# Float32 side matmuls of a fused decoder layer gathered into every second unit of main matmuls, and the last output tile sent in two halves

## The chip, the cores and the metric

The kernel runs on one core of a Trainium2 chip. The metric is the device time of one execution in microseconds (us). A core has TensorE (matmuls, into PSUM banks), VectorE, ScalarE, GpSimd and SyncE; here SyncE does nothing but issue DMAs.

## What is computed

One inference step of a one-layer decoder with three parallel groups of heads, for 256 prompt tokens and 64 sample tokens (8 requests of 8), all in float32:

```python
def finish(x, y_conv, y_swa, y_x, w_out, g_mlp, w_up, w_down):
    x = x + jnp.concatenate([y_conv, y_swa, y_x], axis=-1) @ w_out
    a = jnp.square(jax.nn.relu(rmsnorm(x, g_mlp) @ w_up))
    return x + a @ w_down
...
b, u, q, k, v, qx = mixer_projections(xs, g_mix[l], w_in[l], g_q_swa[l], g_k_swa[l], g_q_x[l])
u_ext = jnp.concatenate([cache_conv[l], u], axis=1)
y_conv = b * short_conv(u_ext, conv_w[l])
y_swa, k_buf, v_buf = swa_sample(q, k, v, cache_swa_k[l], cache_swa_v[l], sinks[l], rel_bias_table)
y_x = cross_attention(qx, cache_mem_k[l], cache_mem_v[l])
s_conv.append(u_ext[:, -(CONV_K - 1):])
xs = finish(xs, y_conv, y_swa, y_x, w_out[l], g_mlp[l], w_up[l], w_down[l])
```

The model width is 2048, the MLP 8192 wide; a head has 128 columns. `y_conv` is a gated convolution over three tokens, `y_swa` attention over a window of 128 tokens (8 heads on 2 key heads), `y_x` attention of 4 heads over 256 memory tokens. The prompt goes through the same layer with its own memory, and its keys and values are outputs. So are the convolution's last two inputs, and the caches of the window moved on by 8 tokens.

## The kernel before

**Main work.** All 320 tokens lie side by side as columns, the model width on partitions. A weight matrix is cut into groups of 512 output columns (four PSUM banks `mm` of 128 rows by 320 columns) and pieces of 512 KB (two blocks of 128 rows). A float32 product is made of three matmuls with shortened operands: a piece arrives in tile `raw` (4 buffers, `load_piece`, SyncE's queue), ScalarE rounds it into `wh`, VectorE makes the rest `wl` = `raw` - `wh` (4 buffers each, `split_piece`); the activations lie in the same two parts, S0h and S0l, S1h and S1l. The right to load the next piece into a `raw` buffer comes with the end of that `wl` split, and the load is issued there in program order.

A **unit** (`run_unit`) is 12 main matmuls of 320 columns (6 of 512 for the memory keys and values). A group has 16 units, or 8 for the half groups of `w_out`. The groups follow in a fixed order: memory queries (C_X), keys and values (C_K), the prompt's memory keys and values, window queries (two groups), the convolution's three parts (C_C, C_H, C_B), then `w_out` in two passes of four half groups, then `w_up` and `w_down` in four rounds of four and four groups. The first pass of `w_out` folds its PSUM banks into the residual x: `pre_out` issues, just before unit 4 of its first half group, four DMAs of 640 KB that bring x into the `lx` tiles, and `part_evac` (VectorE) adds each finished bank to them. The fifth bank, first of the next half group, can be written once the first bank is folded.

**Side work.** Attention, norms and the convolution's leftovers are "jobs": generators that a scheduler (`Side`) advances by a step after each unit (`boundary`: first the evacuations that are due, then the `wl` split, then `side.step()`). `yield n` means "come back n units later". A job waits for its tiles by a model of the engines' times (`Pace`, `after`), and takes a PSUM bank `ax` (four of them) by `bank`. So side matmuls stand in **batches** between two units: plain float32 matmuls, transposes, and those of `cross_sample`, where each head has 32 output rows and the four heads sit in four column tiles of the array. `cross_sample` runs through four requests b for the memory keys and four for the values, each with two loaded tiles of 128x512. All issues of engines are recorded through one helper, so they carry line 166 in the profile; tiles tell them apart.

**What a unit may ask for.** `side.until(needs)` runs extra scheduler steps until the jobs named are done. Unit 4 of the first `w_out` half group asks for "conv" and "convout". The job "convout" makes eight small copies on VectorE and stores them with a DMA on GpSimd. GpSimd's queue keeps program order: behind that store come the two copies of the old window caches, `out_old_k` and `out_old_v` (960 KB each, from DRAM to DRAM, issued by `pre_late`).

**The end.** `down_evac` adds the last banks to x; the tiles of the last group go out one by one on SyncE.

Of the kernel before, what the change touches and what calls it, by code (L numbers as in the profile page):

```python
# [12 lines left out]
ALU = mybir.AluOpType  # L13
AX = mybir.AxisListType

P = 128
D = 2048
KT = 16
# [4 lines left out]
T = TP + TS  # L23
# [224 lines left out]
def trunk_step(ctx: ExitStack, tc: tile.TileContext, I, O):  # L248
    nc = tc.nc
    pace = Pace()  # L250
    side = Side(NW2, pace)
    pace.dram = {a.name for a in list(I.values()) + list(O.values())}
    pe, act, dve = (Paced(pace, n, e) for n, e in (("pe", nc.tensor), ("act", nc.scalar), ("dve", nc.vector)))
    pool, sp = Paced(pace, "pool", nc.gpsimd), Paced(pace, "dma", nc.sync)
# [13 lines left out]
    ax = Slots(axp, "ax", 4, pace.idle)  # L268
# [3 lines left out]
    def after(*tiles):  # L272
        while not pace.ready(tiles):
            yield 1

    def bank():
        return ax.need([P, 512])

    def zt(cols=336):
        return zs.need([P, 336])  # L280

    def sm(n=8):
        return smp.tile([P, 8], F32, name="sm", tag="sm")
# [6 lines left out]
    def half():  # L290
        return w2.need([P, 512])
# [65 lines left out]
    def mean_over(bk, y, scale):  # L357

        hi = yield from zs.need([P, T], F32R)
        lo = yield from zs.need([P, T], F32R)  # L360
        act.activation(out=hi, in_=y, func=AF.Copy)
        dve.tensor_tensor(out=lo, in0=y, in1=hi.bitcast(F32), op=ALU.subtract)
        yield 1
        yield from after(lo)
        pe.matmul(out=bk[:, 0:T], lhsT=scale, rhs=hi, start=True, stop=False)
        pe.matmul(out=bk[:, 0:T], lhsT=scale, rhs=lo, start=False, stop=True)
        yield 1
        zs.put(hi, lo)

    def newton_terms(y, a, mean):  # L370
        act.activation(out=y, in_=mean, func=AF.Ln, bias=eps)
        act.activation(out=y, in_=y, func=AF.Exp, scale=-0.5)
        act.activation(out=a, in_=y, func=AF.Square)
        yield from after(a)
        dve.scalar_tensor_tensor(out=a, in0=mean, scalar=EPS, in1=a, op0=ALU.add, op1=ALU.mult)
# [161 lines left out]
    def mean_rsqrt(out, sq):  # L537

        yield from after(sq)
        bk = yield from bank()  # L540
        yield from mean_over(bk, sq, mean_d)
        y = yield from zt()
        yield from newton_terms(y[:, 0:T], out, bk[:, 0:T])
        ax.put(bk)
        dve.tensor_scalar(out=y[:, 0:T], in0=y[:, 0:T], scalar1=-0.5, scalar2=None, op0=ALU.mult)
        dve.scalar_tensor_tensor(out=out, in0=out, scalar=-3.0, in1=y[:, 0:T], op0=ALU.add, op1=ALU.mult)
        zs.put(y)
# [52 lines left out]
    def start_head(name, ps, gain, dest):  # L600
        early = "rb" not in side.flags
        home = w2 if early else zs
        z = home.must([P, 336])
        if early:
            side.held += 1
            act.activation(out=z[:, 0:T], in_=ps, func=AF.Copy)
        else:
            dve.tensor_tensor(out=z[:, 0:T], in0=ps, in1=rb, op=ALU.mult)

        def gen():  # L610
            if early:
                while "rb" not in side.flags:
                    yield 1
                dve.tensor_tensor(out=z[:, 0:T], in0=z[:, 0:T], in1=rb, op=ALU.mult)
            while side.now < turn[0] or turn[1] == 2:
                yield 1
            turn[0] = side.now + 2
            turn[1] += 1
            y = yield from zt()
            yield from after(z)  # L620
            act.activation(out=y[:, 0:T], in_=z[:, 0:T], func=AF.Square)
            yield 1
            yield from after(y)
            bk = yield from bank()
            yield from mean_over(bk, y[:, 0:T], mean_h)
            a = yield from zt()
            yield from newton_terms(y[:, 0:T], a[:, 0:T], bk[:, 0:T])
            ax.put(bk)
            dve.scalar_tensor_tensor(out=z[:, 0:T], in0=z[:, 0:T], scalar=gain, in1=y[:, 0:T],
                                     op0=ALU.mult, op1=ALU.mult)  # L630
            zs.put(y)
            dest(lambda out, v: dve.scalar_tensor_tensor(out=out, in0=v(a), scalar=-3.0, in1=v(z),
                                                         op0=ALU.add, op1=ALU.mult))
            zs.put(a)
            home.put(z)
            side.held -= int(early)
            turn[1] -= 1

        side.add(name, gen())

    def prompt_cols(t):
# [167 lines left out]
    def cross_sample(f):  # L809
        todo = [(n, b) for n in ("cmk", "cmv") for b in range(4)]  # L810
        queue = []

        def load():
            if todo:
                n, b = todo.pop(0)
                pair = []
                for i in range(2):
                    t = yield from half()
                    src = I[n][f * 4 + b, i]
                    sp.dma_start(out=t, in_=src.rearrange("p h k -> p (h k)") if n == "cmk" else src)  # L820
                    pair.append(t)
                queue.append(pair)

        qm = st["qxm"][f]
        for _ in range(2):
            yield from load()
        sb = yield from bank()
        for b in range(4):
            cur = queue.pop(0)
            yield from after(*cur)  # L830
            for h in range(XH):
                pe.matmul(out=sb[h * 32:(h + 1) * 32, 0:MEM], lhsT=qm[:, h * P + b * 32:h * P + b * 32 + 32],
                          rhs=cur[h // 2][:, (h % 2) * MEM:(h % 2 + 1) * MEM], start=b == 0, stop=b == 3,
                          tile_position=(0, h * 32), skip_group_check=True)
            w2.put(*cur)
            yield from load()
        yield 1
        p = yield from zt()
        den = sm()
        yield from cross_softmax([(p[:, 0:MEM], sb[:, 0:MEM])], den)  # L840
        ax.put(sb)
        yield from after(p)
        pm = []
        for kb in range(2):
            t = yield from half()
            pool.memset(t, 0.0)
            pm.append(t)
        bk = yield from bank()
        for kb in range(2):
            pe.transpose(bk[:, kb * P:(kb + 1) * P], p[:, kb * P:(kb + 1) * P], ident)  # L850
        yield 1
        for kb, t in enumerate(pm):

            dve.tensor_copy(out=bass.AP(tensor=t.tensor, offset=t.offset, ap=[t.ap[0], [P + NS, 4], [32, XH], [1, NS]]),
                            in_=bk[:, kb * P:(kb + 1) * P].rearrange("p (h b t) -> p b h t", h=XH, b=4))
        ax.put(bk)
        zs.put(p)
        yield from after(*pm)
        ob = yield from bank()
        for b in range(4):  # L860
            cur = queue.pop(0)
            yield from after(*cur)
            for kb in range(2):
                for h in range(XH):
                    c = h * 32
                    pe.matmul(out=ob[c:c + 32, 0:P], lhsT=pm[kb][:, b * P + c:b * P + c + 32],
                              rhs=cur[kb][:, h * P:(h + 1) * P], start=b == 0 and kb == 0, stop=b == 3 and kb == 1,
                              tile_position=(0, c), skip_group_check=True)
            w2.put(*cur)
            yield from load()  # L870
        yield 1
        w2.put(*pm)
        o = yield from zt()
        act.activation(out=o[:, 0:P], in_=ob[:, 0:P], func=AF.Copy)
        ax.put(ob)
        yield from after(o)
        bk = yield from bank()
        pe.transpose(bk[:, 0:P], o[:, 0:P], ident)
        yield 1
        zs.put(o)  # L880
        c = TP + f * 32
        yield from put_mix(lambda m: m[:, 12:16, c:c + 32], bk[:, 0:P].rearrange("p (h q) -> p h q", h=XH))
        ax.put(bk)
        w2.put(qm)
        side.held -= 1
# [321 lines left out]
    def down_evac(g, last):  # L1207
        def f(m, ps):
            a = acc[g][:, m, :]
            dve.tensor_tensor(out=a, in0=ps, in1=a, op=ALU.add)  # L1210
            if last and (g == 3 or m == 3):
                c = slice(m, m + 1) if g == 3 else slice(0, 4)
                sp.dma_start(out=O["yT"][:, 4 * g + c.start:4 * g + c.stop, :], in_=acc[g][:, c, :])
        return f
# [44 lines left out]
    bk = ax.must([P, 512])  # L1259
# [74 lines left out]
```

## Time and profile before

| | before |
|---|---|
| median of 3 runs | 1319.12 us (1319.0 to 1320.92) |
| the profiled execution: its time, its span | 1319.92 us, 1317.9 us |
| TensorE busy | 1311.2 us, 99%, 8938 instructions |
| VectorE busy | 669.4 us, 51% |
| ScalarE busy | 538.7 us, 41% |
| GpSimd busy | 17.4 us, 1% |
| granted TensorE clock, mean of the span | 0.999 of full speed |
| read from HBM, written | 211.53 MB, 7.65 MB |

A busy share is an average over the whole span. Side work lies in the first quarter of it, so the stretches (busy time of each engine from one time to another) say more than the table. The chain of waits is the chain of work that ended last, followed back from the end; on TensorE it runs in pieces, main (`mm`) and side (`ax`) by turns. A timeline lists instructions with their start, their duration and, in brackets, the idle time of the engine ahead of them and what ended it. Matmuls of TensorE overlap: one of 320 columns shows some 0.31 us in a timeline, though one starts every 0.147 us.

### The profile page before, as it was taken

To read this page: it belongs to the slowest core of one execution; us is meant where nothing else is said; L and a number is where in the kernel's file an instruction comes from. 1 tells how busy PE (TensorE), PEld (TensorE's weight loads), DVE (VectorE), ACT (ScalarE), POOL (GpSimd) and SP (SyncE) were. 2 spreads that over 40 slices of the span, in tenths; PEclk is the share of its full clock that TensorE was granted. 3 is DMA by queue.
4 is the path that set the end of the run, shared out by engine and by line. 5 is a ranking of instruction groups with operands and counts; after the bars stand their busy time and mean duration, and the time that the engine had idled before them with its cause. 6 is when DMAs were issued, how large, how long until landed. Compare 5 with 4: busy or idle time off the path is not lost.

```text
span 1317.9 us, 21493 instructions
## 1 busy us (share of the span) xinstructions
PE 1311.2 (99%) x8938; PEld 1287.8 (98%) x8938; DVE 669.4 (51%) x1010; ACT 538.7 (41%) x795; POOL 17.4 (1%) x36
## 2 busy tenths in 40 slices
PE   9999999999999999999999999999999999999998
PEld 8988999999999999999999999999999999999998
DVE  6876556776466444444444444344444344444342
ACT  7784544434255344333244432234442224443321
POOL 1011000000000000000000000000000000000000
PEclk9999999999999999999999999999999999999999
DMA  8667564365445444445444444444444443444542
GB/s 313 237 197 258 186 224 149 116 229 208 157 143 163 147 146 142 157 145 162 144 150 139 150 155 159 146 155 132 158 151 156 150 154 129 160 154 152 175 168 73
DMA packets 65024, 217.03 MB, mean 165 GB/s; under 512 B 8373, under 2 KB 10141, under 8 KB 64896
## 3 DMA queue, kind: packets, MB, share of 16 engines
q1 hardware_dynamic: 62896, 210.38, 48.2%
q0 software_dynamic: 1744, 5.19, 1.0%
q8 instruction: 70, 1.15, 0.4%
q14 instruction: 26, 0.21, 0.0%
q10 hardware_dynamic: 288, 0.10, 0.0%
HBM read 211.53 MB, written 7.65 MB: 166 GB/s over the span
## 4 chain that ended last, share of the span: by engine, by line
PE 98%; DVE 1%; DMA 0%; issue 0%; SPq 0%; ACT 0%; DVEq 0%
PE mm L166 95%; PE ax L166 3%; DVE z L166 1%; DMA raw<-in_w_in 0%; DVE lx L166 0%; DVE wl L166 0%; DVE w L166 0%; DVE sm L166 0%; SPq L166 0%; ACT wh L166 0%; DVEq L166 0%
## 5 line engine op out<-in xcount | busy, mean ns | idle before, releaser
L166 DVE TENSOR_TENSOR wl<-raw,wh 128x1024 fp32r<-128x1024 f32 (+1 forms) x361 | 435.9, 1220 | 487.1 <-ACT wh L166 481.5
L166 ACT ACTIVATE wh<-raw 128x1024 fp32r<-128x1024 f32 (+1 forms) x361 | 374.2, 1052 | 642.2 <-PE mm L166 603.9
L166 PE MATMUL mm<-S0h,wh 128*128 128x320 f32 x1472 | 459.9, 312 | 1.2 <-ACT wh L166 1.2
L166 PE MATMUL mm<-S0h,wl 128*128 128x320 f32 x1472 | 455.9, 310 | 0.8 <-DVE wl L166 0.8
L166 PE MATMUL mm<-S0l,wh 128*128 128x320 f32 x1472 | 455.3, 309 | 0.0
L166 PE MATMUL mm<-S1h,wh 128*128 128x320 f32 x1280 | 396.7, 310 | 0.0
L166 PE MATMUL mm<-S1h,wl 128*128 128x320 f32 x1280 | 395.5, 309 | 0.0
L166 PE MATMUL mm<-S1l,wh 128*128 128x320 f32 x1280 | 395.5, 309 | 0.0
L166 PEld LDWEIGHTS mm<-S0h,wh 128*128 128x128 f32 x1472 | 277.0, 188 | 5.4 <-issue 3.5
L166 PEld LDWEIGHTS mm<-S0h,wl 128*128 128x128 f32 x1472 | 276.9, 188 | 1.6 <-DVE wl L166 1.6
L166 PEld LDWEIGHTS mm<-S0l,wh 128*128 128x128 f32 x1472 | 277.0, 188 | 0.2
L166 PEld LDWEIGHTS mm<-S1h,wh 128*128 128x128 f32 x1280 | 240.3, 188 | 0.4 <-issue 0.2
L166 PEld LDWEIGHTS mm<-S1l,wh 128*128 128x128 f32 x1280 | 240.3, 188 | 0.1
L166 PEld LDWEIGHTS mm<-S1h,wl 128*128 128x128 f32 x1280 | 240.3, 188 | 0.0
L166 DVE TENSOR_TENSOR lx<-mm,lx 128x320 f32<-128x320 f32 x96 | 47.0, 490 | 78.1 <-PE mm L166 72.8
L166 ACT ACTIVATE z<-z 128x320 f32<-128x320 f32 (+1 forms) x118 | 54.9, 469 | 62.3 <-DVE z L166 61.2
L166 DVE TENSOR_TENSOR S1l<-z,S1h 128x320 fp32r<-128x320 f32 x68 | 33.4, 491 | 51.6 <-ACT S1h L166 51.6
L166 ACT ACTIVATE S1h<-z 128x320 fp32r<-128x320 f32 x68 | 32.1, 472 | 7.2 <-DVE z L166 5.2
L166 DVE SCALAR_TENSOR_TENSOR z<-mm,r2b 128x320 f32<-128x320 f32 x64 | 31.0, 484 | 0.0
L166 PE MATMUL mm<-wh,S1h 128*128 128x512 f32 x64 | 25.7, 401 | 0.0
L166 PE MATMUL mm<-wh,S1l 128*128 128x512 f32 x64 | 25.1, 392 | 0.0
L166 PE MATMUL mm<-wl,S1h 128*128 128x512 f32 x64 | 25.0, 391 | 0.0
(152 smaller groups left out, 413.7 us busy)
## 6 DMA issues: line engine op xcount, KB each, us to landing
raw<-in_w_up SPq DMA_DIRECT2D x128, 512.0 KB, 3.4
raw<-in_w_down SPq DMA_DIRECT2D x128, 512.0 KB, 3.3
raw<-in_w_in SPq DMA_DIRECT2D x55, 512.0 KB, 3.7
raw<-in_w_out SPq DMA_DIRECT2D x32, 512.0 KB, 3.4
raw<-in_w_mem_k SPq DMA_DIRECT2D x8, 512.0 KB, 5.4
raw<-in_w_mem_v SPq DMA_DIRECT2D x8, 512.0 KB, 3.4
w<-in_cmk SPq DMA_DIRECT2D x16, 256.0 KB, 5.5
w<-in_cmv SPq DMA_DIRECT2D x16, 256.0 KB, 4.8
```

What stands on the lines that cost most here:

```text
L166: return f(*args, **kw)
```

## The change

`bank` gets an argument: by default it now waits until the scheduler's step count is even before it takes a PSUM bank, and looks again only every second step. The two means over squares (`mean_rsqrt`, `start_head`) keep the old way, `bank(1)`. In `cross_sample` the matmuls of each request, keys and values, wait for an even step too. And the very last output tile is added in two halves of 160 columns, the first sent on ScalarE's DMA queue, the second on SyncE's.

```diff
--- before.py
+++ after.py
@@ -273,8 +273,15 @@
         while not pace.ready(tiles):
             yield 1
 
-    def bank():
-        return ax.need([P, 512])
+    def bank(every=2):
+
+        while side.now % every:
+            yield 1
+        t = ax.get([P, 512])
+        while t is None:
+            yield every
+            t = ax.get([P, 512])
+        return t
 
     def zt(cols=336):
         return zs.need([P, 336])
@@ -537,7 +544,7 @@
     def mean_rsqrt(out, sq):
 
         yield from after(sq)
-        bk = yield from bank()
+        bk = yield from bank(1)
         yield from mean_over(bk, sq, mean_d)
         y = yield from zt()
         yield from newton_terms(y[:, 0:T], out, bk[:, 0:T])
@@ -621,7 +628,7 @@
             act.activation(out=y[:, 0:T], in_=z[:, 0:T], func=AF.Square)
             yield 1
             yield from after(y)
-            bk = yield from bank()
+            bk = yield from bank(1)
             yield from mean_over(bk, y[:, 0:T], mean_h)
             a = yield from zt()
             yield from newton_terms(y[:, 0:T], a[:, 0:T], bk[:, 0:T])
@@ -828,6 +835,8 @@
         for b in range(4):
             cur = queue.pop(0)
             yield from after(*cur)
+            while side.now % 2:
+                yield 1
             for h in range(XH):
                 pe.matmul(out=sb[h * 32:(h + 1) * 32, 0:MEM], lhsT=qm[:, h * P + b * 32:h * P + b * 32 + 32],
                           rhs=cur[h // 2][:, (h % 2) * MEM:(h % 2 + 1) * MEM], start=b == 0, stop=b == 3,
@@ -860,6 +869,8 @@
         for b in range(4):
             cur = queue.pop(0)
             yield from after(*cur)
+            while side.now % 2:
+                yield 1
             for kb in range(2):
                 for h in range(XH):
                     c = h * 32
@@ -1207,6 +1218,11 @@
     def down_evac(g, last):
         def f(m, ps):
             a = acc[g][:, m, :]
+            if last and g == 3 and m == 3:
+                for queue, c in ((act, slice(0, T // 2)), (sp, slice(T // 2, T))):
+                    dve.tensor_tensor(out=a[:, c], in0=ps[:, c], in1=a[:, c], op=ALU.add)
+                    queue.dma_start(out=O["yT"][:, KT - 1, c], in_=a[:, c])
+                return
             dve.tensor_tensor(out=a, in0=ps, in1=a, op=ALU.add)
             if last and (g == 3 or m == 3):
                 c = slice(m, m + 1) if g == 3 else slice(0, 4)
```

Three places show how the instructions move. On TensorE, in the memory groups, the scores of the sample tokens against the loaded memory keys of two requests (`w_25` to `w_28` are key tiles, `w_5` the masked queries):

```order
-L166 MATMUL ax_1110<-w_25_1211,w_5_435 32x256 x2
-L166 MATMUL ax_1110<-w_26_1213,w_5_435 32x256 x2
+L166 MATMUL ax_1133<-w_25_1208,w_5_435 32x256 x2
+L166 MATMUL ax_1133<-w_26_1210,w_5_435 32x256 x2
+L166 MATMUL ax_1133<-w_27_1216,w_5_435 32x256 x2
+L166 MATMUL ax_1133<-w_28_1218,w_5_435 32x256 x2
...
-L166 MATMUL ax_1110<-w_27_1219,w_5_435 32x256 x2
-L166 MATMUL ax_1110<-w_28_1221,w_5_435 32x256 x2
```

Two requests, which stood in two batches with a unit between them, stand in one.

On VectorE, at the end of the first `w_out` half group (`lx_3471` is the first x tile, `w_91` and `sm` belong to window scores), before:

```order
L166 TENSOR_SCALAR w_91_3287<-w_91_3287,sm 128x128 x2
L166 TENSOR_TENSOR wl<-raw,wh 128x1024
L166 TENSOR_TENSOR lx_3471<-mm,lx_3471 128x320
```

and now (`w_88` and `lx_1376` are the eight copies of "convout", `lx_3450` is the first x tile):

```order
L166 TENSOR_TENSOR wl<-raw,wh 128x1024
L166 COPY w_88_3430<-lx_1376 128x2
L166 COPY w_88_3430<-lx_1376 128x16
...
L166 TENSOR_SCALAR z_3400<-z_3400,sm 128x192
L166 TENSOR_TENSOR S1l<-ax_3375,S1h 128x2x128
L166 TENSOR_TENSOR lx_3450<-mm,lx_3450 128x320
```

The eight copies, which stood some 40 instructions earlier, now stand behind the last `wl` split ahead of the first fold.

On SyncE, the loads at the same place (`sk_d`: window bias, `in_csk` and `in_csv`: a cached window, `in_xT`: x), before:

```order
L166 DMA w_86_3161<-sk_d 128x2x256
L166 DMA raw<-in_w_out 128x1024 x2
L166 DMA w_89_3265<-in_csk 128x512
L166 DMA w_90_3267<-in_csv 128x512
L166 DMA raw<-in_w_out 128x1024 x4
L166 DMA lx_3471<-in_xT 128x1280
```

and now:

```order
L166 DMA raw<-in_w_out 128x1024 x3
L166 DMA w_89_3443<-sk_d 128x2x256
L166 DMA w_90_3445<-in_csk 128x512
L166 DMA w_91_3447<-in_csv 128x512
L166 DMA lx_3450<-in_xT 128x1280
```

Three loads of side jobs stand directly ahead of the x loads. GpSimd's order is the same as before.

## Rows read from the trace of the kernel before

**Rows 1.** Stretches; columns: us, each engine's busy us (instructions), clock, DMA share, GB/s.

```profile
8.00:332.00 324.00, 323.45 (x2219) 301.23 (x2220) 222.55 (x472) 175.19 (x349) 17.25 (x32) 0.99 0.62 211
332.00:1300.00 968.00, 968.00 (x6602) 968.00 (x6602) 440.44 (x523) 358.31 (x440) 0.00 (x0) 1.00 0.46 151
```

**Rows 2.** Chain of waits, pieces by time; columns: start, us, what.

```profile
99.64 1.00 PE ax L166 x16
...
111.30 0.57 PE ax L166 x8
...
131.29 1.01 PE ax L166 x32
...
139.97 0.86 PE ax L166 x4
...
202.41 1.44 PE ax L166 x20
203.84 1.96 PE mm L166 x12
...
304.07 0.87 PE ax L166 x8
...
306.71 1.29 PE ax L166 x6
```

**Rows 3.** Timeline of VectorE, group C_H; columns: start, us, instruction [idle before].

```profile
252.20 0.49 DVE L166 TENSOR_TENSOR z<-mm,rb 128x320 f32<-128x320 f32 x1
...
266.56 1.22 DVE L166 TENSOR_TENSOR wl<-raw,wh 128x1024 fp32r<-128x1024 f32 x1
```

**Rows 4.** Timeline of TensorE, in C_H and at the second `w_out` group.

```profile
267.84 0.42 PE L166 MATMUL mm<-S0h,wl 128*128 128x320 f32 x1 [0.48 <-DVE wl L166]
...
309.59 0.40 PE L166 MATMUL mm<-S1h,wh 128*128 128x320 f32 x1
```

**Rows 5.** Timeline of ScalarE, first `w_out` group.

```profile
299.61 1.06 ACT L166 ACTIVATE wh<-raw 128x1024 fp32r<-128x1024 f32 x1 [1.66 <-issue]
```

**Rows 6.** Timeline of VectorE, C_B to the first fold.

```profile
285.13 0.68 DVE L166 COPY w<-lx 128x2 f32<-128x2 f32 x8
...
302.79 1.22 DVE L166 TENSOR_TENSOR wl<-raw,wh 128x1024 fp32r<-128x1024 f32 x1
...
309.04 0.49 DVE L166 TENSOR_TENSOR lx<-mm,lx 128x320 f32<-128x320 f32 x1 [5.02 <-DMA lx<-in_xT]
```

**Rows 7.** Timeline of SyncE's queue (issues).

```profile
273.95 0.42 SPq L166 DMA_DIRECT2D w<-in_csk  x1
...
274.89 0.59 SPq L166 DMA_DIRECT2D w<-sk_d  x1
...
304.04 0.33 SPq L166 DMA_DIRECT2D raw<-in_w_out  x1
304.42 1.93 SPq L166 DMA_DIRECT2D lx<-in_xT  x4
```

**Rows 8.** DMA issues of the page; last column: median us to landing.

```profile
raw<-in_w_out SPq DMA_DIRECT2D x32, 512.0 KB, 3.4
```

**Rows 9.** Timeline of GpSimd's queue.

```profile
286.11 0.54 POOL L166 DMA_DIRECT2D out_conv<-w  x1 [107.70 <-DVE w L166]
286.65 0.60 POOL L166 DMA_DIRECT2D out_old_k<-in_cache_swa_k  x1
287.25 0.57 POOL L166 DMA_DIRECT2D out_old_v<-in_cache_swa_v  x1
```

**Rows 10.** Tile `raw`, the one load issued at 288.12.

```profile
DMA to landing us min/median/max: 8.8/8.8/8.8
```

**Rows 11.** Two stretches at the start; columns as in the first group.

```profile
5.00:8.00 3.00, 1.53 (x5) 0.78 (x5) 2.38 (x4) 2.25 (x5) 0.00 (x0) 0.99 0.96 340
8.00:11.40 3.40, 3.32 (x12) 3.33 (x13) 2.26 (x4) 1.54 (x3) 0.00 (x0) 0.51 1.03 415
```

**Rows 12.** Timeline of VectorE, the last add.

```profile
1314.38 0.49 DVE L166 TENSOR_TENSOR lx<-mm,lx 128x320 f32<-128x320 f32 x1 [1.27 <-PE mm L166]
```

## The prediction, made before the changed kernel ran

> **What bounds the kernel now.** I read the stretches first [rows 1]. From 332 to 1300 us TensorE is busy all the time: 6602 matmuls in 968.00 us, 0.1466 us each. Nothing in that part is touched, except the very end. From 8 to 332 us, where all side work lies, TensorE is idle for only 0.55 us. So the kernel is bound by TensorE, and the edit can win in two ways alone: by making TensorE's own stretch of side matmuls shorter, or by removing that half microsecond of waits. It can lose by any new wait of TensorE. Next I read the chain of waits for what a side batch costs, and last the places where VectorE, SyncE's queue and GpSimd's queue come close to TensorE's need.
>
> **What a batch costs.** In the chain a batch has a piece of its own, and some batches also stretch the main piece behind them beyond 0.1466 us per matmul [rows 2]. The batch at 139.97 (two full-width matmuls of 256 columns) takes 0.86 us. The batch at 202.41 is such a pair plus one batch entry of memory values (eight matmuls of 32 columns in four column tiles): 1.44 us, and the 12 main matmuls at 203.84 take 1.96 us where 12 x 0.1466 = 1.76, so 1.64 in all. The column-tiled part is thus 1.64 - 0.86 = 0.78 us. Two batch entries together, at 131.29, take 1.01 us plus the same tail of 0.20, so 1.21 us, and not 2 x 0.78 = 1.56. Putting two column-tiled runs together saves 0.35 us. For memory keys the rows say the same: 0.57 us for one entry at 111.30, 1.00 for two at 99.64, so 2 x (0.57 + 0.20) - (1.00 + 0.20) = 0.34. Full-width matmuls show no such fixed part: 0.86 is the same alone or within a longer batch.
>
> **What the edit gives there.** By the order of instructions the 64 batches (warm-up left out) become 57, but only column-tiled runs count. Key runs go from 7 to 4 and value runs from 5 to 4. Against that, one run of window scores that stood right behind a value run stands alone now: 1 lost. Net 3 runs: 3 x 0.34 = **-1.0 us**. If the fixed part held for every batch it would be 7 x 0.34 = 2.4 us, a rival below.
>
> **The wait in C_H.** While VectorE works through the four folds of group C_H, weight split wl comes so late that TensorE sits idle 0.48 us ahead of 267.84 [rows 4]; that is nearly all of the 0.55 us that it idles from 8 to 332 [rows 1]. VectorE was busy from 252.20 to 266.56 without a pause [rows 3]: four folds, and between them a scaling and maximum of 512 columns and three normalisations of window scores. In the new order two smaller scalings and maxima stand there instead, while the piece is needed no earlier. So the wait goes: **-0.55 us** (bounds -0.6 and 0). The splits behind it were not waited for.
>
> **The new wait, at the first w_out group.** This is the large term. The four DMAs that bring the residual x go out on SyncE just before unit 4 of the first w_out group, and VectorE's first fold needs the first of them. In the trace VectorE waits 5.02 us for it, to 309.04 [rows 6], and TensorE starts the first unit of the second group at 309.59 [rows 4]: it needs the PSUM bank that the fold frees, and comes just in time. There is no slack to give away.
>
> I measure from the start of the third wh split of that group, at 299.61 [rows 5], which TensorE itself releases.
> - TensorE reaches the second group 309.59 - 299.61 = 9.98 us later. Of that 0.87 and 1.3 us are side batches (at 304.07 and 306.71) [rows 2]. In the new order only two transposes stand there, about 0.2. So TensorE would arrive at 9.98 - 0.87 - 1.3 + 0.2 = 8.0 us.
> - The wl split ends at 302.79 + 1.22 = 304.01 in the trace [rows 6], 4.4 us after the mark, since VectorE was behind. In the new order the score work comes earlier, so it takes wh (1.0 us) and wl (1.22) and two handovers of some 0.1: 2.4 us.
> - SyncE then issues the raw load (0.38 us to the next issue) and the first x load. In the new order three more loads stand between, because the extra step of the side scheduler that "convout" now asks for also starts two other jobs: 0.42, 0.42 and 0.59 us [rows 7] and gaps, 1.55 us. The x load landed 309.04 - 304.42 = 4.6 us after its issue. So it lands at 2.4 + 0.4 + 1.55 + 4.6 = 9.0 us, up to 0.4 later if the 768 KB ahead of it move no faster than 640 KB in 1.6 us, the step from the raw load's landing to x's (304.04 + 3.4 to 309.04) [rows 6 to 8].
> - The fold and the start behind it take 309.59 - 309.04 = 0.55: TensorE starts at 9.55 to 9.95 and waits **1.5 to 1.9 us**.
>
> Then GpSimd. Its queue holds, in this order, the store of conv and the two copies of the old caches (960 KB each, DRAM to DRAM), and it stands waiting for the eight copies of "convout" [rows 9]. In the trace they ran at 285.13, so the big copies went out at 286.65 and 287.25, when nothing urgent was queued. In the new order the eight copies (0.68 us [rows 6]) stand behind the wl split above: the cache copies go out about 1.5 and 2.1 us after that split, and the x load 1.95 us after it. They meet. The row that shows the price: the raw load issued 0.87 us after the second cache copy took 8.8 us to land [rows 10], where its kind takes 3.4 [rows 8], 5.4 more. The bounds are 0 (x gets ahead of the copies) and 5.4. I take 5.0, near that row, because x's rows also queue behind three loads while the copies' rows start.
>
> The Trainium skill (DMA: Bandwidth & Descriptors, section Queues, rings and completion order) says that a DMA engine takes its queues in turn, a packet from each. By that rule x would get turns between the large rows; but the row of 8.8 us shows a load that got none, and with turns it would still need several, so the sum by the rule is a wait some 2 us shorter.
>
> Together TensorE waits 1.7 + 5.0 = **6.7 us** (1.5 to 7.3). Nothing later in the group is then late: its other splits and x loads are spaced as before.
>
> **The clock.** From 5 to 8 us TensorE was busy only 1.53 of 3 us, and from 8 to 11.4 the granted clock was 0.51 (1.2 GHz) although it was busy [rows 11]; half of 3.4 us was lost. After 6.7 idle us I expect the same: **+1.7 us** (0 to 3). The Trainium skill (TensorE: Matmul & The Clock Gate, section HAM oscillation) says that a DMA wait of TensorE amid a kernel puts it back to the slow clock; no row of this trace shows that mid-kernel.
>
> **The last tile.** The last add takes 0.49 us for 320 columns [rows 12]. In halves the second ends about as late as now (two instructions, a start more), and its DMA leaves as late. 0, with 0.3 either way; cover is none, it all counts.
>
> **Sum.** -1.0 - 0.55 + 6.7 + 1.7 = +6.85. The profiled execution took 1319.92 us (span 1317.9 and 2.0 around it), 0.8 over the median of 1319.12. On the median: **1325.9 us**.
>
> **Rivals.**
> 1. The x loads meet the copies little or not. Wait 1.5 to 4 us, the clock holds: -1.55 + 1.5 to 4 gives 1319.1 to 1321.6, same. For it: x is issued before the second copy. Against: the 8.8 us row.
> 2. Faster: the fixed part of 0.34 us is paid by every batch, 7 x 0.34 = 2.4, and 0.55 in C_H, and x lands in time: 1316.2. It decides if the x load lands within 7.5 us of the mark. Against it: full-width batches show no fixed part, and my lowest landing is 9.0.
> 3. The order does not do what it says, so that unit parity is lost after the extra scheduler step: column-tiled runs still pair, so only 0.3 us hangs on it.
>
> **Chances.** Forecast (copies met, wait 5 to 7.3, clock loss 0 to 3; 1322.5 to 1328) 0.66; rival 1 0.21; rival 2 0.08; worse than all, over 1328.5, 0.05. The range from 1319.0 to 1328.2 leaves out rival 2, part of the worst, and little else. A measurement here can tell about 0.2%, 2.6 us. Faster 0.07, same 0.24, slower 0.69.
>
> **What would show it.** In the profile after: an idle stretch of TensorE of 5 to 7 us at about 305 us, released by VectorE's fold of x, which itself waits for the x DMA; GpSimd's two cache copies issued within a microsecond of the x load; a granted clock near 0.5 right behind. In C_H no wait for wl. If TensorE shows no gap there, or one below 2 us, my landing time is wrong. If it is faster by more than 2 us, the fixed cost of a batch is.

## The result and the profile after

The changed kernel takes 1329.91 us (median of 4 runs, 1329.24 to 1330.82) against 1319.41 for the kernel before (4 runs): a ratio of 1.0076 with a 95% interval of 1.0064 to 1.0088, so 10.5 us slower. The prediction had the direction and the place, but said 1325.9 with a range to 1328.2: too small by 4 us.

| | before | after |
|---|---|---|
| the profiled execution: its time, its span | 1319.92, 1317.9 us | 1330.82, 1328.7 us |
| TensorE busy | 1311.2 us | 1313.3 us |
| VectorE, ScalarE busy | 669.4, 538.7 us | 669.7, 540.0 us |
| granted clock, mean of the span | 0.999 | 0.995 |

The timeline of TensorE shows the end of the first `w_out` half group and the first matmul of the second (start, us, instruction, idle ahead of it):

```profile
307.01 0.31 PE L166 MATMUL mm<-S1h,wl 128*128 128x320 f32 x1
316.10 0.61 PE L166 MATMUL mm<-S1h,wh 128*128 128x320 f32 x1 [8.78 <-DVE lx L166]
```

A matmul starts every 0.147 us, so the second should have started at 307.15: TensorE stands still for 8.95 us. (The bracket gives 8.78, because it counts from the modelled end of the matmul ahead.) In the kernel before it started without a wait [rows 4]. VectorE's timeline says why; the rows answer to [rows 6]:

```profile
300.21 1.23 DVE L166 TENSOR_TENSOR wl<-raw,wh 128x1024 fp32r<-128x1024 f32 x1 [2.48 <-ACT wh L166]
301.35 0.68 DVE L166 COPY w<-lx 128x2 f32<-128x2 f32 x8
...
315.46 0.49 DVE L166 TENSOR_TENSOR lx<-mm,lx 128x320 f32<-128x320 f32 x1 [12.48 <-DMA lx<-in_xT]
```

The first fold waits 12.48 us for the x load, where it was 5.02. The eight copies of "convout" stand behind the last `wl` split ahead of it. The two queues at that place, SyncE's and GpSimd's, answer to [rows 7, 9]:

```profile
301.84 0.43 SPq L166 DMA_DIRECT2D w<-sk_d  x1
302.32 0.46 SPq L166 DMA_DIRECT2D w<-in_csk  x1
302.88 0.38 SPq L166 DMA_DIRECT2D w<-in_csv  x1
303.30 2.28 SPq L166 DMA_DIRECT2D lx<-in_xT  x4
```

```profile
302.32 0.54 POOL L166 DMA_DIRECT2D out_conv<-w  x1 [124.34 <-DVE sm L166]
302.86 0.60 POOL L166 DMA_DIRECT2D out_old_k<-in_cache_swa_k  x1
303.46 0.58 POOL L166 DMA_DIRECT2D out_old_v<-in_cache_swa_v  x1
```

Three side loads stand ahead of x, and x is issued at 303.30, between the two cache copies. The DMA view of the stretch from 290 to 325 us gives the sizes and the median time from issue to landing of each kind:

```profile
lx<-in_xT SPq DMA_DIRECT2D x4, 640.0 KB, 13.6
out_old_k<-in_cache_swa_k POOLq DMA_DIRECT2D x1, 960.0 KB, 10.2
out_old_v<-in_cache_swa_v POOLq DMA_DIRECT2D x1, 960.0 KB, 10.0
w<-sk_d SPq DMA_DIRECT2D x1, 256.0 KB, 3.8
w<-in_csk SPq DMA_DIRECT2D x1, 256.0 KB, 5.3
w<-in_csv SPq DMA_DIRECT2D x1, 256.0 KB, 10.6
```

`in_csv`, issued 0.02 us after the first copy, lands with the copies (313.48); x lands at 315.37, 1.9 us after both. The load issued just ahead of the copies, `in_csk`, took half the time. Last, the stretches (columns as in [rows 1]): the wait, the time behind it, and the rest of the kernel.

```profile
307.10:316.10 9.00, 0.22 (x3) 0.03 (x1) 0.64 (x2) 1.28 (x2) 0.00 (x0) 0.75 0.89 352
316.10:321.90 5.80, 5.80 (x28) 5.19 (x29) 5.73 (x11) 0.00 (x0) 0.00 (x0) 0.50 0.91 323
323.00:1300.00 977.00, 977.00 (x6668) 975.59 (x6667) 448.45 (x550) 362.92 (x456) 0.00 (x0) 1.00 0.46 151
```

The granted clock had fallen within the wait (0.75 on its mean). TensorE then works for 5.8 us at 1.2 GHz, so 2.9 us are lost there; from 323 us on nothing waits any more.

In group C_H the wait for `wl` of [rows 4] is gone, but another of the same size has come, inside a side batch of the long kind that the even step makes (eight score matmuls and four transposes between two units; its last transposes wait for VectorE's softmax):

```profile
261.48 1.89 PE L166 MATMUL ax<-kT,qT 128*128 128x256 f32 x8
263.41 0.44 PE L166 MATMUL ax<-ident,z 128*128 128x128 f32 x2
264.42 0.43 PE L166 MATMUL ax<-ident,w 128*128 128x128 f32 x2 [0.57 <-DVE w L166]
```

The cost of the batches is worked out from the trace as the time from the main matmul ahead of a batch to the second one behind it, less two steps of 0.147 us, less waits. For all batches from 50 us on it is 50.51 us in 62 batches before. After, it is 50.98 in 55. One of these, at 319.43, ran at half the clock and cost 2.4 us; the same batch at full clock, in the run below with the copies moved, cost 1.2. Without these 1.2 us it is 49.8: a gain of 0.7.

The difference of 10.9 us between the two profiled executions is then 8.95 (wait) + 2.9 (clock) - 0.7 (batches) + 0.0 (C_H) - 0.1 (from the start of the last main matmul to the end, 3.74 us instead of 3.83), in sum 11.05.

### The profile page after: what moved, and what is told of

Its sections match the earlier page's. It is cut to its first block, busy times and chain, and to the rows that moved or that the text cites. A ratio compares the mean times of both kernels' runs of the same rounds, so it can differ in the third digit from the quotient of the medians.

```text
span 1328.7 us, 21498 instructions
## 1 busy us (share of the span) xinstructions
PE 1313.3 (99%) x8938; PEld 1290.7 (97%) x8938; DVE 669.7 (50%) x1011; ACT 540.0 (41%) x795; POOL 17.5 (1%) x36
## 4 chain that ended last, share of the span: by engine, by line
PE 97%; DVE 1%; DMA 1%; SPq 0%; issue 0%; ACT 0%; DVEq 0%; ACTq 0%
PE mm L166 93%; PE ax L166 3%; DMA lx<-in_xT 1%; DVE z L166 1%; DMA raw<-in_w_in 0%; DVE wl L166 0%; DVE lx L166 0%; SPq L166 0%; DVE sm L166 0%; ACT wh L166 0%; DVE S1l L166 0%; DVE w L166 0%; DVEq L1346 0%; DVEq L166 0%; ACTq L166 0%
## 5 line engine op out<-in xcount | busy, mean ns | idle before, releaser
L166 DVE TENSOR_TENSOR lx<-mm,lx 128x320 f32<-128x320 f32 (+1 forms) x97 | 46.9, 486 | 85.6 <-PE mm L166 73.0
```

Of the source, the lines that this page charges most:

```text
L166: return f(*args, **kw)
```

## The experiments

Theory A: the loss is x's landing behind the side loads and the cache copies, and the change gains some 0.7 to 0.8 us in the batches. Rival B: the copies do not matter, only x's later issue. Rival C: the longer batches of the even step cost the time. Rival D: every batch fewer saves something, whatever is in it. Ratios are to the kernel before, timed on the same chip. All edits are on the changed kernel unless said otherwise. "The mark" is, as in the prediction, the start of the third `wh` split of the first `w_out` half group.

### Is it the copies?

**The copies moved away**

```diff
         for n in ("k", "v"):
-            pool.dma_start(out=O[f"old_{n}"]...
+            sp.dma_start(out=O[f"old_{n}"]...
```

> The changed kernel, but the two copies of the old window caches leave on SyncE's queue at the second pass of w_out, some 50 us later, instead of on GpSimd's queue behind the store of conv; all else stands as changed. Theory A (TensorE's idle 8.95 us at the first fold is the copies: in the changed kernel they went out at 302.86 and 303.46, x at 303.30, and x landed 1.9 us after the second copy had): x lands some 4.6 us after its issue as in the kernel before, TensorE waits 1 to 2 us, the granted clock stays up, and the median is 0 to 2 us over the kernel before. Rival B (x is late because of the three side loads ahead of it on its own queue and its later issue): the wait stays near 9 us and the median near +10.5.

1323.43 us, 1.0029 (1.0020 to 1.0038): +3.5. The wait shrinks from 8.95 to 3.37 us, counted the same way (the matmul ahead starts at 307.24). The rows are TensorE's first matmul of the second group, and the stretches of the wait and behind it:

```profile
310.76 0.38 PE L166 MATMUL mm<-S1h,wh 128*128 128x320 f32 x1 [3.21 <-DVE lx L166]
```

```profile
307.50:310.70 3.20, 0.05 (x1) 0.00 (x0) 0.57 (x2) 1.12 (x2) 0.00 (x0) 1.00 0.98 388
310.70:313.00 2.30, 2.23 (x16) 2.27 (x16) 2.30 (x5) 0.00 (x0) 0.00 (x0) 1.00 1.00 412
```

Rival B falls as the whole cause: the copies hold 5.6 us of x's landing (16.26 us after the mark with them, 10.68 without). But a wait is left that they did not make, and Theory A's 1 to 2 us for it was too low. Without the copies x still takes 6.5 us from its issue, not 4.6. The last of the three loads ahead of it lands at 308.40, and x 1.63 us behind that, at 310.03. By the packet records of the trace the three loads take 2.65 us of all 16 DMA engines: 256 packets of 47 ns and 256 of 118 ns on the mean. The medians are 46 and 84 ns, which would make 2.1 us; the rest is a few packets of up to 1.2 us, and what held those was not traced. The clock stayed at 1.00 in this execution; the ten runs have mean clocks from 0.996 to 1.0.

**One copy moved away**

```diff
-            pool.dma_start(out=O[f"old_{n}"]...
+            (pool if n == "k" else sp).dma_start(out=O[f"old_{n}"]...
```

> As the run before, but only the copy of the old values is moved; that of the keys stays on GpSimd at its place. Theory A, with the two copies lasting 10.6 us together from the first issue to the last landing: one copy alone lands about 5 us earlier, x behind it too, TensorE waits 3 to 5 us; the median is +2 to +6 over the kernel before, depending on whether the clock falls after so short a wait. Rival B: +10.5. If x gets turns between the rows of a copy, the wait is under 3 us.

1328.52 us, 1.0063 (1.0048 to 1.0078): +8.6, a miss. One copy holds x nearly as long as two:

```profile
315.41 0.61 PE L166 MATMUL mm<-S1h,wh 128*128 128x320 f32 x1 [6.95 <-DVE lx L166]
```

The packet records fit it. They hold queue, size, start and length of each packet on the 16 engines; worked out from them:

```
kernel                     packets of the copies  mean us   first start  last end
changed                    32 of 61,440 bytes     2.34      306.85       312.82
one copy moved             16 of 61,440 bytes     2.34      307.55       312.90
rows of 5 KB (below)       384 of 5,120 bytes     0.20      306.21       318.73
```

Of the one copy's packets 8 at most were in flight at a time, of the two copies' 16 at most: one copy is two rounds of 2.34 us on half of the engines, two copies are two rounds on all of them, and either way the last packet is through 5.4 to 6 us after the first has begun. x is there only when its last row is. The shares of the DMA view show it, for the one copy from 307.5 to 312.9 (q0 is GpSimd's queue, q1 SyncE's; packets, MB, share of 16 engines):

```profile
q1 hardware_dynamic: 318, 1.20, 56.3%
q0 software_dynamic: 41, 0.99, 43.7%
```

and for the changed kernel from 306.8 to 312.3:

```profile
q0 software_dynamic: 66, 1.97, 85.3%
q1 hardware_dynamic: 118, 0.35, 17.4%
```

**Shorter rows**

```diff
-            pool.dma_start(out=O[f"old_{n}"].rearrange("b t g d -> b (t g d)"),
-                           in_=I[f"cache_swa_{n}"][0, :, 8:128].rearrange("b t g d -> b (t g d)"))
+            pool.dma_start(out=O[f"old_{n}"].rearrange("b (c t) g d -> c b (t g d)", t=5),
+                           in_=I[f"cache_swa_{n}"][0, :, 8:128].rearrange("b (c t) g d -> c b (t g d)", t=5))
```

> The changed kernel, but each cache copy is described in rows of 5 KB instead of 60 KB; bytes, queue and place stay. The trace of the changed kernel has the 32 packets of the copies at 2.3 us each, and between two of them an engine took one packet of SyncE's queue (0.12 to 0.21 us). If the length of the packet is what makes x wait (Theory A with turns by packet), x now gets about half of the engines' time, lands some 2 to 3 us earlier, TensorE waits 5 to 7 us, and the median is +5 to +9 against the kernel before. If the copies' bytes go first whatever their packets, the wait stays at 8 to 9.5 us and the median at +9 to +11.5.

1327.81 us, 1.0057 (1.0042 to 1.0072): +8.0, and a wait of 7.05 us instead of 8.78 (both by the bracket), at the edge of the 5 to 7 us that turns by packet were to give. The two queues now share the engines evenly from 306.8 to 312.3:

```profile
q1 hardware_dynamic: 269, 1.10, 50.7%
q0 software_dynamic: 274, 1.12, 50.2%
```

So the queues are served in turn, packet by packet. In the changed kernel the records show the turns too: between the two rounds of the copies, from 308.1 to 311.6 us, 15 packets of SyncE's queue start on the 16 engines, about one on each. The Trainium skill (DMA: Bandwidth & Descriptors, section Queues, rings and completion order) says so too: a DMA engine takes a whole packet from one queue before it goes to the next. The trace agrees, and adds the price of a turn: 2.34 us for a packet of 60 KB, against which SyncE's turn of one packet lasts 0.08 to 0.20 us (medians).

### Is it the place of x in the queue?

**The side loads behind x**

```diff
-    ..., needs=qn + [f"k{g}", f"v{g}", "bias", "mix"], ...
+    ..., needs=qn + [f"k{g}", f"v{g}", "bias", "mix"] + ["xgo"] * (g * i), ...
-    ..., needs=qn + [f"k{g}", f"v{g}", "biass"], ...
+    ..., needs=qn + [f"k{g}", f"v{g}", "biass"] + ["xgo"] * (g * i), ...
     def pre_out(*groups):
         ...
+        side.flags.add("xgo")
```

> The changed kernel, but the two window jobs whose three loads stood directly ahead of x may start only once the x loads are issued. convout and the cache copies stay as late as in the changed kernel. The first x load then leaves about 1 us ahead of the first cache copy instead of 0.44 us behind it. Theory A with its queue part as the runs so far have it (a load issued 1 us ahead of the copies lands in 4.7 us, one issued behind them waits for them): x lands about 7 us after the mark, TensorE does not wait or waits under 0.5 us, and the median is -1.5 to +0.5 against the kernel before. If the two copies delay x whatever its place, the wait stays above 4 us.

1324.23 us (1322.70 to 1327.71), 1.0038 (1.0026 to 1.0051): +4.5, a miss, though its first half came true. x is issued at 303.17, 1.03 us ahead of the first copy, and lands in 4.86 us; at the first fold TensorE loses 0.3 us at most (its matmuls start at 308.33 and 308.75). The side loads now stand behind the copies in x's place, and one of them makes TensorE wait (this is of the longest of the five executions):

```profile
322.19 0.66 PE L166 MATMUL ax<-w,qs 128*32 128x128 f32 x8 [2.89 <-DMA w<-in_csk]
```

```profile
320.50:324.00 3.50, 1.81 (x13) 1.42 (x14) 1.23 (x1) 1.22 (x2) 0.00 (x0) 0.67 1.04 418
324.00:328.00 4.00, 4.00 (x17) 4.00 (x16) 1.15 (x3) 0.00 (x0) 0.00 (x0) 0.50 0.54 193
```

The clock fell here too. The loss went to the next load in line. (1.7 us of this execution's loss are not x's: the clock also fell from 34.96 to 38.38 us, behind a wait of 1.26 us for `in_c_hot`.)

**Both moved**

```diff
-            pool.dma_start(out=O[f"old_{n}"]...
+            sp.dma_start(out=O[f"old_{n}"]...
...
+    (the edits of the run before as well)
```

> The changed kernel with both edits of the earlier runs: the cache copies leave on SyncE's queue some 50 us later, and the two window jobs whose loads stood ahead of x start behind the x loads. The x loads stay where the change put them. If the loss is the sum of what shares the DMA engines with x at that place (Theory A), then with x alone there no wait is left, neither of the fold for x (8.95 us in the changed kernel, 3.2 with the copies moved) nor of a window score for its cached keys (2.9 with the side loads moved alone): -1.5 to +0.5 us against the kernel before, as with the early x loads (-1.4). If something else of the new order costs, +1 us or more with no such wait.

1319.90 us against 1319.58, 1.0003 (0.9994 to 1.0012). Neither long wait is left and the clock holds. The time is in the range expected. The batches cost 50.0 us, 0.5 less than before, but that gain does not show in the time: side work runs later and TensorE waits 0.7 us for ScalarE in a late side batch (at 362.80), 0.57 in C_H as the changed kernel does, and 0.3 at the first fold, which still waits for x.

**"convout" early**

```diff
-        cu = yield from half()
+        cu = cuo
...
-        w2.put(cu)
...
-            side.add("convout", conv_out_job(), cost=1)
+            side.add("convout", conv_out_job())
+    cuo = const.tile([P, 72], F32, name="cuo")
```

> The changed kernel, but convout copies into a small tile of its own and needs no slot of the shared pool, so the scheduler runs it as soon as C_H is done: by the order of instructions some 70 instructions of VectorE earlier, and the cache copies leave with it, some 30 us ahead of the x loads. Two side loads still stand ahead of x, at 118 ns for each of their 256 packets on 16 engines about 1.9 us. Theory A: x lands about 9.5 us after the start of the third wh split of that group, TensorE is there after 8.0 and needs 0.7 more, so it waits 0.5 to 2.5 us, the clock holds, and the median is -0.5 to +1.5 against the kernel before. Rival C: +2 us or more with the wait gone.

1321.65 us (1320.41 to 1323.08), 1.0015 (1.0006 to 1.0024): +1.8, a little over the range. The wait is 2.29 us, as expected, but the clock fell behind it in this execution:

```profile
308.87 0.38 PE L166 MATMUL mm<-S1h,wh 128*128 128x320 f32 x1 [2.29 <-DVE lx L166]
```

```profile
308.90:311.00 2.10, 2.10 (x11) 2.10 (x12) 2.03 (x6) 0.00 (x0) 0.00 (x0) 0.73 1.00 417
311.00:313.00 2.00, 2.00 (x10) 2.00 (x9) 1.90 (x7) 0.65 (x3) 0.00 (x0) 0.50 0.93 336
```

Of its eleven runs, the five with a mean clock of 0.999 or more have a median of 1320.85, the six at 0.998 one of 1322.5. The mean clock of a run does not say where the clock fell, so how many of the six fell behind the wait is not shown: four of the eleven runs with x loaded earlier (below), whose trace has no wait there, have 0.998 as well.

**"convout" late, in the kernel before**

```diff
-            side.add("convout", conv_out_job(), cost=1)
+            side.add("convout", conv_out_job(), needs=("outgo",), cost=1)
...
+        if "convout" in un["needs"]:
+            side.flags.add("outgo")
         n = side.until(un["needs"])
```

> The kernel before, with one edit: convout may not start until unit 4 of the first w_out half group asks for it. Nothing is paired, no side load moves ahead of x. The store of conv and the two cache copies then leave about 1 us behind the first x load, not 0.4 us ahead of it. Theory A: the delay of convout by itself makes a wait; how long depends on whether x, issued first, is overtaken: 0 to 3 us if not (median 0 to +3), 6 to 9 us (median +6 to +11) if the copies take it all the same. Rivals B and C: no wait, within 1 us of the kernel before.

1320.42 us against 1319.92, 1.0004 (0.9995 to 1.0013), with no wait of TensorE at the place: "0 to 3 if not overtaken" it was. The queues:

```profile
303.91 1.99 SPq L166 DMA_DIRECT2D lx<-in_xT  x4
```

```profile
304.94 0.60 POOL L166 DMA_DIRECT2D out_old_k<-in_cache_swa_k  x1
305.53 0.57 POOL L166 DMA_DIRECT2D out_old_v<-in_cache_swa_v  x1
```

The first x load leaves 1.03 us ahead of the first copy and lands in 4.7 us. So the delay of "convout" alone costs nothing that can be told; the changed kernel loses because the three side loads push x behind the copies, and by their own bytes.

**Only the pairs of `cross_sample`**

```diff
-    def bank(every=2):
-
-        while side.now % every:
-            yield 1
+    def bank(every=1):
+
         t = ax.get([P, 512])
```

> The changed kernel without the even step in bank (every job takes its bank as before); cross_sample's pairs and the halved last tile stay. In its order of instructions the eight copies of convout stand as late as in the changed kernel, behind the last wl split ahead of the first fold, and three side loads stand ahead of x. Theory A: the pairs alone push convout back, so the loss is there in full: an idle stretch of TensorE of 7 to 9 us at the first fold, +8 to +11 over the kernel before. Rival C (the loss comes from the long batches that the even step makes): within 2 us of the kernel before.

1324.23 us, 1.0032 (1.0021 to 1.0043): +4.3, half of what was expected. The pairs alone push "convout" back, so Rival C falls, but x is issued 0.85 us ahead of the first copy here (301.63 and 302.48): 107 packets of x rows start before the first packet of the copies (307.17), and x lands at 312.46, ahead of the copies. TensorE waits 4.66 us.

### What the change is worth without the wait

**Three x tiles loaded four units earlier**, in the changed kernel and in the kernel before

```diff
-                  pre={1: lambda: pre_out(0, 1, 2, 3)} if g == 0 else None)
+                  pre={0: lambda: pre_out(0, 1, 2), 1: lambda: pre_out(3)} if g == 0 else None)
```

> The changed kernel, but three of the four x tiles are loaded at the head of the first w_out half group, four units earlier; the fourth stays where it was. convout, the two cache copies and the three side loads stay as late as in the changed kernel. Theory A (all that the change loses, it loses because x lands behind the side loads and the cache copies): no idle stretch of TensorE at the first fold, no fall of the granted clock, and the change shows only what it gains: about 0.8 us in the batches and 0.15 at the end, so -2 to +0.5 us against the kernel before. Rival C (the longer batches and the order of side work cost by themselves): +1 us or more with no idle stretch.

> The kernel before with the same earlier load of three x tiles: there the fold waited for x but TensorE did not. Both theories: within 0.7 us of the kernel before. The run stands beside the one with the change, so that their difference is the change without the wait.

The changed kernel with the edit: 1318.48 us, 0.9987 (0.9978 to 0.9996), the fastest of all. The kernel before with it: 1319.50, 0.9998 (0.9989 to 1.0007). The view of TensorE's waits for the former has no fold in it (us in total, times, longest):

```profile
PE ax L1277 <- DVE ones L166: 1.1, 1, 1.1
PE ax L166 <- DVE w L166: 0.6, 1, 0.6
PE ax L166 <- DMA w<-in_c_hot: 0.6, 1, 0.6
PE mm L166 <- ACT wh L166: 0.5, 1, 0.5
```

The side loads, "convout" and the copies stand as late as in the changed kernel. So all of the loss was x's landing, and what the change gains is about 1 us by the medians: its batches cost 49.44 us instead of 50.51. The two profiled executions alone would not tell (1318.81 and 1318.80): the former lost more at its start, 0.56 us in a wait for `in_c_hot` at 33 us and two main matmuls of 0.147 us in the first 20 us. Both vary with the execution: that wait is 1.3 us in the run that alters the last tile alone, and absent in the kernel before.

**Pairs only, with the early x loads**

```diff
-        while side.now % every:
-            yield 1
...
-                  pre={1: lambda: pre_out(0, 1, 2, 3)} if g == 0 else None)
+                  pre={0: lambda: pre_out(0, 1, 2), 1: lambda: pre_out(3)} if g == 0 else None)
```

> The pairs of cross_sample and the halved last tile, without the even step in bank, and with three x tiles loaded four units earlier, so that nothing waits at the first fold. Theory A (the gain in the batches comes from column-tiled runs that are put together, nearly all of them cross_sample's): -0.5 to -1.5 us against the kernel before, as the whole change with the early x loads has (-1.4). Rival D (each batch fewer saves something): there are 69 batches against 64 before and 57 with the even step, so +0.5 or more against the whole change with early x loads by 12 batches at 0.1 us, that is -0.2 or worse.

1319.51 us against 1319.77, 1.0001 (0.9992 to 1.0010). By the time this lies between the two answers, nearer to Rival D's, but the trace speaks against Rival D's reason. There are 68 batches (counted from 50 us on), 6 more than before, and they cost 50.04 us, 0.47 less. What has gone is in other places: TensorE waits 1.2 us for `wl` splits, where before it was 0.55 in C_H. The batches that hold column-tiled matmuls are 19 before, 18 here, and 15 in the whole change with the early x loads (16 in the changed kernel itself). Here there are 6 batches more, 1 of this kind fewer, and 0.47 saved; there 7 fewer, 4 of this kind fewer, and 1.07 saved. Solved for two prices, that is an estimate of 0.3 us for a batch with column-tiled matmuls and of nothing for a batch as such. The run with the copies moved was not used for it and bears it out: with 55 batches, 16 of this kind, the estimate says 49.75 us and its trace has 49.76. The even step does bring some of them together, which the expectation had put down to `cross_sample` alone.

**Only the halved last tile**, on the kernel before

```diff
+            if last and g == 3 and m == 3:
+                for queue, c in ((act, slice(0, T // 2)), (sp, slice(T // 2, T))):
...
+                return
```

> The kernel before with the halved last tile alone. Theory A: from the last main matmul to the end of the span the profile shows 3.87 us before and 3.70 with the change, so 0 to -0.3 us, below what the times can tell. Rival: the second queue's first use at the end costs a start, up to +0.5.

1319.92 us against 1319.86, 1.0001 (0.9992 to 1.0009): nothing that can be told.

## Why the prediction was wrong

By the steps of its sum, in the profiled executions:

| step | predicted | measured |
|---|---|---|
| batches | -1.0 | -0.7 (-1.07 without the wait) |
| wait in C_H | -0.55 | 0.0 |
| TensorE's arrival, after the mark | 8.0 | 8.04 |
| end of the `wl` split, issue of x, after the mark | 2.4, 4.35 | 2.32, 4.19 |
| x landed without the copies | 9.0 to 9.4 | 10.68 |
| the copies on top | 5.0 | 5.6 |
| from landing to TensorE's start | 0.55 | 0.73 |
| wait | 6.7 | 8.95 |
| clock | 1.7 | 2.9 |
| last tile | 0 | -0.1 |

**Right** were the direction, the place, the chain (copies of "convout", GpSimd's queue, x, fold, PSUM bank), the arrival of TensorE and the issue of x to 0.2 us, and that only column-tiled runs pay when they are put together (16 such batches instead of 19, as counted). The rivals fell: x did meet the copies, the fixed part is not paid by every batch, and the order did what it says.

**The step that failed** is "the new wait", in two terms that were sized too small; the mechanism was right.
- *x without the copies.* The prediction took x's time from issue to landing from the kernel before, 4.6 us, and let the three loads ahead of it cost only the time to issue them, with 0.4 us in reserve for their bytes. That priced their 768 KB like x rows, at 1.9 us. Their packets took 2.65 us of all engines, and the last of them landed 9.05 us after the mark, and the raw load ahead of them lands at 5.8 (2.4 + 3.4; 5.77 in the changed kernel), so the three took 3.25 us. The step from there to x is 1.63 us, as the prediction had it. The run without the copies has x 10.68 us after the mark, 1.3 over the upper bound: all of that lies in the three loads.
- *The copies.* 5.0 us against 5.6: the row of 8.8 us that it came from was the right one, and its 5.4, given as a bound, was 0.2 short of what happened. A rule without a surcharge fits both kernels: the load behind the copies lands when they have landed, plus about its own time (296.9 and 1.1 us after the copies in the kernel before; 315.37 and 1.9 us after them in the changed one). But it would not have saved the prediction. With the 8.6 us that the second copy takes from issue to landing in the kernel before, it puts x some 14.7 us after the mark (4.5 + 8.6 + 1.6), where the prediction had 14.0 to 14.4; the runs have 16.26, for the copy took 10.0 us here.

The sentence that by turns the wait would be some 2 us shorter was wrong as a price, though the turns are real, as the packet records and the run with short rows show. And the three loads did not come from the extra scheduler step, as was said: they start in the ordinary step behind the fourth unit, in which "convout" starts as well, because two window jobs had just given back their slots.

**The clock** was within its bounds (0 to 3), but the value was taken from a stretch of 3.4 us at the start [rows 11], and TensorE worked longer at the low clock here, 5.8 us.

**C_H**: the wait for `wl` went as predicted, and what came in its place was not looked for. The longer batches of the even step hold transposes that wait for VectorE's softmax, 0.57 us.

The range's upper end had both terms of x at their bounds (a wait of 7.3 us), full clock loss, and C_H as won. The landing without the copies lay 1.3 us outside its bound, the copies 0.2 and the start behind the landing 0.2, and the 0.55 of C_H was not won: that is what carried the time beyond 1328.2.

## What to carry to other kernels

A load that is needed soon must be issued ahead of large copies and of other loads, however small the step: x behind three small loads and 0.44 us behind a copy made a wait of 9 us, behind the loads and 0.85 us ahead of the copies one of 4.7 us, 1.03 us ahead of both 0.3 at most. Before an edit that shifts side jobs, list what shares the DMA engines with each load that has no slack, and price it as the landing of what is ahead of it plus its own time. Take that landing from a place where the DMA engines are as busy, since the same copy took 8.6 us at one place and 10.0 at another. And when such a load is the weak place, issue it earlier: that alone turned a loss of 10.5 us into a gain of 1.4.

## What the runs showed of the hardware

- One DRAM-to-DRAM copy of 960 KB in rows of 60 KB holds a load up nearly as long as two (a wait of TensorE of 6.95 us against 8.78): 16 packets of 2.34 us in two rounds on half of the engines. The first packet of the copies starts 4.0 us after the issue in the changed kernel (302.86 and 306.85) and 1.4 us after it in the kernel before (286.65 and 288.04); why the former is longer was not tried.
- A packet of 2048 bytes of the cached windows took 84 ns and one of x with 5120 bytes 196 ns, both medians in the changed kernel, so 24 and 26 bytes per ns on an engine. The mean of the former is 118 ns where the loads stand ahead of x, for a few take up to 0.9 us (1.2 with the copies moved), and 84 ns where they stand behind it.
- The length of TensorE's wait does not settle by itself whether the clock falls. By the brackets of the profiled executions it fell to 0.50 at waits of 1.26 us (with the side loads behind x, from 34.96 us on), 2.29 and 2.89 us, stayed at 1.00 at 1.32, 1.55 and 3.21 us, and fell at 4.66, 6.95, 7.05 and 8.78 us (mean clocks of these four 0.997 to 0.995). The Trainium skill (TensorE: Matmul & The Clock Gate, section HAM oscillation) names DMA waits amid a kernel as what puts TensorE back to the slow clock; the trace agrees on that. What decides at the shorter waits stays open.
- The start varies with the execution, whatever the kernel. Main matmuls start every 0.25 us or slower at first (in ten of the fourteen profiled executions every 0.267 us for a while, the step at 1.2 GHz) and every 0.147 us (2.4 GHz) from somewhere between 7 and 13.6 us on; 69 to 87 of them start in the first 20 us. That alone is up to 2.6 us between two executions, as large as some of the effects above. The kernel before and the changed kernel have 76 each, so their comparison is free of it.
